# Band attention on one Trainium2 core: a fixed round order on three engines, the division a round later, low parts on GpSimd

## The chip, the cores and the metric

One core of one Trainium2 chip runs the whole program, launched once. The metric is device time in microseconds (us). The matrix engine is TensorE (PE; its weight loads are PEld), the others are VectorE (DVE), ScalarE (ACT) and GpSimd (POOL); SyncE (SP) issues the DMAs.

## The reference

One step of a hybrid encoder layer on 2048 prompt frames and 8 running streams of 16 frames. A combined projection feeds three mixers: band attention (8 heads of 64), a delta-rule mixer and a diagonal state-space mixer. Their outputs go through one output projection and a layer norm, then through a feed-forward block. The part at issue is the attention:

```python
def one_chunk(c):                      # prompt: 64 queries, their own chunk and the 8 chunks before
    s = jnp.einsum('bqhd,bkhd->bhqk', qc, kc) * scale + bias
    s = jnp.where(valid, s, NEG_INF)
    p = jax.nn.softmax(s, axis=-1)
    return jnp.einsum('bhqk,bkhd->bqhd', p, vc)

def band_attention_sample(q, k, v, k_cache, v_cache, table):   # 8 streams, 512 + 16 keys
    s = jnp.einsum('bqhd,bkhd->bhqk', q, kk) * d_h ** -0.5 + rel_bias(table, rel)
    return jnp.einsum('bhqk,bkhd->bqhd', jax.nn.softmax(s, axis=-1), vv)
```

## The kernel before

The program has stages: the combined projection; the mix stage, in which the state-space part (product `s5p`, L1020) ends; the attention; the output projection with its norm; the feed-forward block. The attention is the stretch from 913 to 1254 us of the trace.

A float32 product on PE is made from two parts of an operand: a high part, which is a cast to the type fp32r, and a low part, which is the operand minus its high part. So each 128-row block of queries and keys needs casts and subtractions before PE can take it.

`attention` (L1071) walks over 16 tiles of 128 queries, each with four pairs of heads: 64 rounds. A tile sees `nk` = min(i+1, 5) blocks of 128 keys. For a round:

- `a_scores` (L1160): for each of the two heads, and for each key segment (one segment up to tile 3, then mostly two, since keys lie in tiles of four blocks), PE multiplies high and low queries with the keys into a PSUM tile `aps` (L1184, L1185; four such tiles exist). DVE adds the bias `nb` and keeps a running extremum in `st` (`tensor_tensor_reduce`, below TTR, L1186; in the trace `CUSTOM_DVE_ANT_0` and a `DVE_READ_ACCUMULATOR2_ANT` behind it). ACT takes the exponential of a whole head and sums it (L1189, an `ACTIVATE` and its read of the accumulator). In the same function DVE inverts the two sums (L1191) and multiplies both heads (L1194, `TENSOR_SCALAR`, below TS).
- `a_values` (L1197): PE transposes the weights block by block (L1212) into `tps` tiles (three exist); the copies to `PT` go to ACT and DVE in turn (L1215, L1217); PE multiplies with the values (L1220) into the one PSUM tile `aob`; behind a tile's fourth pair ACT copies it out (L1223).

`a_values` is called `AHEAD` = 2 rounds behind `a_scores`. `a_tile` loads and splits the queries of a tile (casts on ACT L1155, L1156; low part `qlz` on DVE L1157). `a_kblock` does it for four key blocks at once (cast on ACT L1133, low part on DVE L1134). In tiles 1 to 8 `a_sample` does the attention of one running stream: scores (L1269), TTR (L1270), exponential (L1272), division (L1273, L1274), transposes (L1278), copy of `sPT` on ACT (L1279), then 20 short value products in a burst into the same `aob` tile (16 at L1289 and 4 at L1290), and two DVE copies into `sos` (L1293). In tiles 2 to 9 `w_part` splits an eighth of the output weights: two ACT casts (L61) and two DVE subtractions (L62).

The order on each engine is not the order of the text. A scheduler places instructions by priority and readiness: the order written is a preference, and an instruction that is ready later is passed by others. Each engine then runs its own list strictly in order.

Of the kernel before, what the change touches and what calls it, by code (L numbers as in the profile page):

```python
# [30 lines left out]
AHEAD = 2  # L31
# [11 lines left out]
class K:  # L43
# [1027 lines left out]
    def attention(self, es):  # L1071
# [17 lines left out]
        self.kst, self.vt = {}, {}  # L1089
# [6 lines left out]
        todo = []  # L1096
        for i in range(16):
            t = self.a_tile(i)
            for p in range(4):
                todo.append((t, p, self.a_scores(t, p)))  # L1100
                if len(todo) > AHEAD:
                    self.a_values(*todo.pop(0))
            if 2 <= i <= 9:
                self.w_part(i - 2)
            if 1 <= i <= 8:
                self.a_sample(i - 1)
                if i == 8:
                    nc.sync.dma_start(self.mixT[0:512, SEQ:NT].rearrange("(f p) t -> p f t", p=128), self.sos)

        w0 = c.tile([128, 5, 8, 128], F32, name="w0", tag="nb")  # L1110
        for x in todo:
            self.a_values(*x)
# [4 lines left out]

    def tsplit(self, parts, t):
        src, sl = self.at_a(parts, t)
        return src[:, sl].rearrange("(f p) t -> p f t", p=128)  # L1120

    def a_kblock(self, b):

        nc = self.nc
        ks = self.ak.tile([128, 8, 512], F32R, name="kst", tag="kst")
        for i in range(4):
            kr = self.ak.tile([128, 4, 128], F32, name="kr", tag="kr", bufs=2)
            nc.sync.dma_start(kr, self.tsplit(self.kT, b * 4 + i))
            ts = slice(i * 128, (i + 1) * 128)
            for q in range(2):  # L1130
                r, o = slice(q * 64, q * 64 + 64), slice(64 - q * 64, 128 - q * 64)
                hi = ks[r, q::2, ts]
                nc.scalar.copy(hi, kr[r])  # L1133
                nc.vector.tensor_tensor(ks[o, q::2, ts], kr[r], hi.bitcast(F32), OP.subtract)  # L1134
        self.kst[b] = ks

    def a_tile(self, i):

        nc = self.nc
        V = nc.vector  # L1140
        aw = self.aw
        b, r = divmod(i, 4)
        if r == 0:
            self.a_kblock(b)
        v = aw.tile([128, 512], F32, name="vt", tag="vt", bufs=6)
        vsrc, sl = self.at_a(self.vS, i)
        nc.sync.dma_start(v, vsrc[sl])
        self.vt[i] = v
        qr = aw.tile([128, 4, 128], F32, name="qr", tag="qr", bufs=2)
        nc.sync.dma_start(qr, self.tsplit(self.qT, i))  # L1150
        qd = aw.tile([128, 8, 128], F32R, name="qd", tag="qd")
        ql = self.qlz[i % 2]
        for q in range(2):
            rr, o = slice(q * 64, q * 64 + 64), slice(64 - q * 64, 128 - q * 64)
            nc.scalar.copy(qd[rr, q::2], qr[rr])  # L1155
            nc.scalar.copy(qd[o, q::2], qr[rr])  # L1156
            V.tensor_tensor(ql[rr, q::2], qr[rr], qd[rr, q::2].bitcast(F32), OP.subtract)  # L1157
        j0 = max(0, i - 4)
        return dict(i=i, qd=qd, ql=ql, vt=[self.vt[j] for j in range(j0, i + 1)], kst=dict(self.kst), ob=None)

    def a_scores(self, t, p):

        nc = self.nc
        V, mm = nc.vector, nc.tensor.matmul
        aw = self.aw
        i, qd, ql, kst = t["i"], t["qd"], t["ql"], t["kst"]
# [6 lines left out]
        for q in range(2):  # L1173
# [4 lines left out]
            if n1:  # L1178
                segs.append((kst[b - 1], min(512 - 128 * n1, 320), 512, 512 - 128 * n1, 0, 128 * n1))
            segs.append((kst[b], 0, max(128 * n2, 192), 0, 128 * n1, 128 * n2))  # L1180
            low = 3e38
            for ks, c0, c1, d0, x0, n in segs:
                ps = self.asp.tile([128, 512], F32, name="aps", tag="s")
                mm(ps[:, c0:c1], qd[:, h], ks[:, h, c0:c1], start=True, stop=False)  # L1184
                mm(ps[:, c0:c1], ql[:, h], ks[:, h, c0:c1], start=False, stop=True)  # L1185
                V.tensor_tensor_reduce(x[:, x0:x0 + n], ps[:, d0:d0 + n], nb[:, x0:x0 + n], 1.0, low,  # L1186
                                       OP.add, OP.min, st[:, q:q + 1])
                low = st[:, q:q + 1]
            nc.scalar.activation(x, x, AF.Exp, scale=-1.0, bias=st[:, q:q + 1], accum_out=st[:, 2 + q:3 + q])  # L1189
        rs = aw.tile([128, 2], F32, name="rs", tag="ars", bufs=4)  # L1190
        V.reciprocal(rs, st[:, 2:4])  # L1191
        for q in range(2):
            x = P[:, q, 0:128 * nk]
            V.tensor_scalar(x, x, rs[:, q:q + 1], None, OP.mult)  # L1194
        return P

    def a_values(self, t, p, P):  # L1197
        nc = self.nc
        V, mm = nc.vector, nc.tensor.matmul
        aw = self.aw  # L1200
        i, vt = t["i"], t["vt"]
        nk = len(vt)
        if t["ob"] is None:
            t["ob"] = self.aop.tile([128, 4, 128], F32, name="aob", tag="o")
        ob = t["ob"]
        PT = aw.tile([128, 10, 128], F32, name="PT", tag="PT")
        units = [(q, j) for j in range(nk) for q in range(2)]
# [627 lines left out]
```

## Time and profile before

| what | us |
|---|---|
| device time, median of three runs (lowest, highest) | 2910.81 (2909.86, 2921.8) |
| device time of the profiled execution | 2915.03 |
| its span, first to last instruction | 2913.2 |
| mean granted TensorE clock over the span | 0.986 of full speed |
| attention stage, 915.4 to 1254 | 338.6 |

The profile is one execution. A table of stretches gives an engine's busy time and the granted clock in each; a timeline gives an engine's instructions in order, and in brackets how long the engine stood idle before one and what released it; the waits sum such idle time by the line that ended it.

### The profile page before, as it was taken

Reading aid. Unit: us, or ns where it says so; the run is one execution under the profiler, and the core shown is the slowest. Engines: PE = TensorE matmul, PEld = TensorE weight load, DVE = VectorE, ACT = ScalarE, POOL = GpSimd, SP = SyncE. Lnnn points to the kernel's source line nnn. Section 1 sums busy time; section 2 is a strip of 40 time slices with the busy share of each in tenths; the row PEclk is TensorE's granted clock in tenths of the full one; section 3 lists DMA queues with packets and bytes.
Section 4 is the critical chain, followed back from the end, with each engine's and each line's share of the span. In section 5 each row is a group of like instructions: output and inputs, shape, how many; then the busy total and the mean of one; then the engine's idle time right before and its main releaser. Section 6 shows DMA issues by size and latency. Waiting matters only on the chain.

```text
span 2913.2 us, 46312 instructions
## 1 busy us (share of the span) xinstructions
PE 2795.9 (96%) x16677; PEld 2447.0 (84%) x16677; DVE 1963.9 (67%) x4972; ACT 1319.0 (45%) x2735; POOL 1001.0 (34%) x906
## 2 busy tenths in 40 slices
PE   8999999989999999999999999999999999999998
PEld 8988888867777777778889899888989988888887
DVE  7587887797764667968855555565555556566666
ACT  3554454343456556722244344354434435444443
POOL 0011111241100000002454444446554554776774
PEclk9999999999999889999999999999999999999999
DMA  5644444464557442144542122143222214322321
GB/s 183 202 107 121 111 129 121 134 171 133 165 182 220 142 138 61 50 159 159 179 157 76 58 71 75 58 165 141 100 73 78 97 66 156 145 98 94 113 83 58
DMA packets 292428, 351.88 MB, mean 121 GB/s; under 512 B 85586, under 2 KB 218534, under 8 KB 291878
## 3 DMA queue, kind: packets, MB, share of 16 engines
q1 hardware_dynamic: 292198, 348.92, 37.9%
q8 instruction: 131, 2.15, 0.3%
q14 instruction: 99, 0.81, 0.1%
HBM read 276.58 MB, written 74.89 MB: 121 GB/s over the span
## 4 chain that ended last, share of the span: by engine, by line
PE 47%; POOL 6%; DMA 3%; DVE 2%; ACT 2%; issue 1%; SPq 0%; DVEq 0%; ACTq 0%; POOLq 0%
PE fdp L67 7%; PE fdp L68 7%; PE fdp L66 7%; POOL wu L1482 2%; DMA wur<-in_w_upL 2%; PE wops L66 2%; PE wops L67 2%; PE wops L68 2%; PE fupz L68 2%; PE fupv L66 2%; PE fupv L68 2%; PE fupv L67 2%; PE fupz L66 2%; PE fupz L67 2%; PE fupx L66 2%; PE fupx L67 2%
## 5 line engine op out<-in xcount | busy, mean ns | idle before, releaser
L1482 POOL TENSOR_TENSOR wu<-wur,wu 128x512 fp32r<-128x512 f32 x315 | 420.3, 1338 | 556.7 <-ACT wu L1481 544.3
L1600 DVE TENSOR_TENSOR fy<-fy,fdp 128x512 f32<-128x512 f32 x500 | 342.2, 686 | 268.5 <-PE fdp L68 266.9
L66 PE MATMUL fdp<-wdh,hh 128*128 128x512 f32 x1020 | 397.7, 390 | 2.0 <-DVE fy L1600 1.9
L1481 ACT CAST wu<-wur 128x512 fp32r<-128x512 f32 x315 | 194.1, 617 | 448.7 <-DMA wur<-in_w_upL 202.8
L68 PE MATMUL fdp<-wdh,hl 128*128 128x512 f32 x1020 | 397.1, 389 | 0.0
L67 PE MATMUL fdp<-wdl,hh 128*128 128x512 f32 x1020 | 397.1, 389 | 0.0
L66 PE MATMUL pps<-xh,wh 128*128 128x384 f32 (+2 forms) x800 | 280.6, 352 | 10.0 <-ACT xh L61 8.7
L67 PE MATMUL pps<-xl,wh 128*128 128x384 f32 (+2 forms) x800 | 279.3, 349 | 2.1 <-DVE xl L62 2.0
L68 PE MATMUL pps<-xh,wl 128*128 128x384 f32 (+2 forms) x800 | 277.5, 348 | 0.4 <-DVE wl L62 0.3
L66 PEld LDWEIGHTS fdp<-wdh,hh 128*128 128x128 f32 x1020 | 191.4, 188 | 41.7 <-DVE fy L1600 3.7
L68 PEld LDWEIGHTS fdp<-wdh,hl 128*128 128x128 f32 x1020 | 191.5, 188 | 40.3 <-DVE hl L1547 0.2
L67 PEld LDWEIGHTS fdp<-wdl,hh 128*128 128x128 f32 x1020 | 191.5, 188 | 37.9 <-DVE wdl L62 0.2
L1547 DVE TENSOR_TENSOR hl<-fre,hh 128x384 fp32r<-128x384 f32 (+1 forms) x180 | 155.4, 864 | 89.8 <-ACT hh L1546 88.1
L61 ACT CAST wdh<-wdr 128x1024 fp32r<-128x1024 f32 x94 | 98.5, 1050 | 207.3 <-PE fdp L68 205.0
L66 PEld LDWEIGHTS pps<-xh,wh 128*128 128x128 f32 x800 | 152.1, 191 | 22.0 <-ACT xh L61 9.7
L67 PEld LDWEIGHTS pps<-xl,wh 128*128 128x128 f32 x800 | 152.0, 190 | 14.0 <-DVE xl L62 5.1
L68 PEld LDWEIGHTS pps<-xh,wl 128*128 128x128 f32 x800 | 151.8, 190 | 11.7 <-issue 1.8
L62 DVE TENSOR_TENSOR wl<-wr,wh 128x512 fp32r<-128x512 f32 (+1 forms) x152 | 104.7, 695 | 61.4 <-ACT wh L61 60.6
L62 DVE TENSOR_TENSOR wdl<-wdr,wdh 128x1024 fp32r<-128x1024 f32 x94 | 133.4, 1421 | 15.7 <-ACT wdh L61 15.7
L1447 POOL TENSOR_TENSOR fxc<-fxs 128x256 f32<-128x256 f32 x17 | 19.2, 1129 | 321.4 <-ACT fxs L1443 321.4
L61 ACT CAST wh<-wr 128x512 fp32r<-128x512 f32 (+1 forms) x152 | 92.5, 619 | 80.1 <-DMA wr<-in_w_inA 41.4
L1542 ACT ACTIVATE fre<-fre,ld_b_up 128x384 f32<-128x384 f32 (+1 forms) x144 | 85.9, 597 | 74.3 <-DVE fre L1551 48.4
(555 smaller groups left out, 7410.7 us busy)
## 6 DMA issues: line engine op xcount, KB each, us to landing
wdr<-in_w_dnL SPq DMA_DIRECT2D x96, 512.0 KB
wur<-in_w_upL SPq DMA_DIRECT2D x92, 512.0 KB
wr<-in_w_inA SPq DMA_DIRECT2D x70, 512.0 KB
TU<-tD SPq DMA_DIRECT2D x34, 256.0 KB
y<-in_x SPq DMA_DIRECT2D x17, 512.0 KB
x<-y SPq DMA_DIRECT2D x17, 512.0 KB
fxr<-x SPq DMA_DIRECT2D x17, 512.0 KB
fy<-x SPq DMA_DIRECT2D x17, 512.0 KB
```

The lines of the kernel that those rows point to most:

```text
L61: nc.scalar.copy(hi, src)
L62: nc.vector.tensor_tensor(lo, src, hi.bitcast(F32), OP.subtract)
L66: mm(out, lh, rh, start=first, stop=False, **kw)
L67: mm(out, lh, rl, start=False, stop=False, **kw)
L68: mm(out, ll, rh, start=False, stop=last, **kw)
L1447: P.tensor_tensor(b["T1"], b["B12"], b["B11"], OP.subtract)
L1481: self.nc.scalar.copy(hi, src)
L1482: P.tensor_tensor(lo, src, hi.bitcast(F32), OP.subtract)
L1542: nc.scalar.activation(r, src, AF.Relu, bias=self.bu[:, c * 2 + i:c * 2 + i + 1])
L1547: V.tensor_tensor(hl, r, hh.bitcast(F32), OP.subtract)
L1600: V.tensor_tensor(y, y, ps[x], OP.add)
```

## The change

What it does, in six parts:

1. The helpers `mm`, `turn`, `dve` and `act` put each attention instruction of PE, DVE and ACT behind the instruction that was written before it for the same engine (`behind`, with `issue_after`). So from the second round on these three engines run the order of the text. `w_part` and GpSimd's work are not pinned themselves.
2. A round k is written so: division of round k-1 (`a_norm`), scores of k, values of k-2 (`a_values`), transposes and copies of k-1 (`a_turn`).
3. The low parts of queries and keys go from DVE to GpSimd (`a_queries`, `a_keys`).
4. Key tiles are two fixed ones; a key block is loaded and split one block a tile, two tiles ahead, where four came at once. Queries come one tile ahead.
5. The sample's work is spread over its tile: scores at p = 0, division behind that round's scores, transposes at p = 1, the value burst at p = 2 before that round's scores. The caches of the next stream are loaded as soon as the last ones were read.
6. The copy of a tile's result, the casts and the exponentials keep their engines.

```diff
-                todo.append((t, p, self.a_scores(t, p)))
-                if len(todo) > AHEAD:
-                    self.a_values(*todo.pop(0))
-            if 2 <= i <= 9:
-                self.w_part(i - 2)
-            if 1 <= i <= 8:
-                self.a_sample(i - 1)
+                if p == 0:
+                    if i < 14:
+                        self.a_load_k(i + 2)
+                    if i < 15:
+                        self.a_load_q(i + 1)
+                elif p == 1 and i < 14:
+                    self.a_keys(i + 2)
+                elif p == 2 and i < 15:
+                    t1 = self.a_tile(i + 1)
+                    self.a_queries(t1, 0)
+                elif p == 3 and i < 15:
+                    self.a_queries(t1, 1)
+                if rounds:
+                    self.a_norm(rounds[-1])
+                if streams and p == 0:
+                    sample = self.s_scores(b)
+                    if b < 7:
+                        self.s_load_k(b + 1)
+                if streams and p == 2:
+                    self.s_values(b, sample)
+                    if b < 7:
+                        self.s_load_v(b + 1)
+                rounds.append(self.a_scores(t, p))
+                if streams and p == 0:
+                    self.s_norm(sample)
+                if len(rounds) > 2:
+                    self.a_values(rounds.pop(0))
+                if len(rounds) > 1:
+                    self.a_turn(rounds[0])
+                self.pinned = True
+                if streams and p == 1:
+                    self.s_turn(sample)
+                if p == 3 and 2 <= i <= 9:
+                    self.w_part(i - 2)
...
+    @contextmanager
+    def behind(self, engine):
+        last = next((i for i in reversed(self.nc.cur_bb.bb.instructions) if i.engine == engine), None)
+        if not self.pinned or last is None:
+            yield
+        else:
+            with self.tc.issue_after(last):
+                yield
+    def dve(self, f, *a, **kw):
+        with self.behind(mybir.EngineType.DVE):
+            getattr(self.nc.vector, f)(*a, **kw)
...
+    def a_keys(self, i):
+        kr, ks = self.ld_["k", i], self.kst[i // 4 % 2]
+        ts = slice(i % 4 * 128, i % 4 * 128 + 128)
+        for q in range(2):
+            r, o = slice(q * 64, q * 64 + 64), slice(64 - q * 64, 128 - q * 64)
+            hi = ks[r, q::2, ts]
+            self.act("copy", hi, kr[r])
+            self.nc.gpsimd.tensor_tensor(ks[o, q::2, ts], kr[r], hi.bitcast(F32), OP.subtract)
+    def a_queries(self, t, q):
+        qr, qd = self.ld_["q", t["i"]], t["qd"]
+        rr, o = slice(q * 64, q * 64 + 64), slice(64 - q * 64, 128 - q * 64)
+        self.act("copy", qd[rr, q::2], qr[rr])
+        self.nc.gpsimd.tensor_tensor(t["ql"][rr, q::2], qr[rr], qd[rr, q::2].bitcast(F32), OP.subtract)
+        self.act("copy", qd[o, q::2], qr[rr])
...
+    def a_norm(self, s):
+        P, st = s["P"], s["st"]
+        rs = self.aw.tile([128, 2], F32, name="rs", tag="ars", bufs=4)
+        self.dve("reciprocal", rs, st[:, 2:4])
+        for q in range(2):
+            x = P[:, q, 0:128 * s["nk"]]
+            self.dve("tensor_scalar", x, x, rs[:, q:q + 1], None, OP.mult)
```

The three places below are those on which the steps of the prediction rest. In the rows `ISA` is a TTR (with `aps` among its inputs) or its accumulator read. First DVE in one of the late tiles, before:

```order
L1191 RECIPROCAL rs<-st 128x2
L1186 ISA P,st<-aps,nb,st 128x384
L1186 ISA st 128x1
L1194 TENSOR_SCALAR P<-P,rs 128x640 x2
L1186 ISA P,st<-aps,nb,st 128x384
L1186 ISA st 128x1
L1217 COPY PT<-tps 128x512
L1157 TENSOR_TENSOR qlz_11564<-qr,qd 64x4x128
L1191 RECIPROCAL rs<-st 128x2
L1194 TENSOR_SCALAR P<-P,rs 128x640 x2
```

and now (the helper gives all of them one line, L1186):

```order
L1186 RECIPROCAL rs<-st 128x2
L1186 TENSOR_SCALAR P<-P,rs 128x640 x2
L1186 ISA P,st<-aps,nb 128x256
L1186 ISA st 128x1
L1186 ISA P,st<-aps,nb,st 128x384
L1186 ISA st 128x1
L1186 ISA P,st<-aps,nb 128x256
L1186 ISA st 128x1
L1186 ISA P,st<-aps,nb,st 128x384
L1186 ISA st 128x1
L1186 COPY PT<-tps 128x512
```

The low part has left the engine, and the division always stands ahead of all four TTRs of the next round, with the copy at the end. Second, PE around a sample's value burst in tiles 4 to 8, before:

```order
L1220 MATMUL aob<-PT,vt 64x128 x4
L1184 MATMUL aps<-kst,qd 128x512
L1220 MATMUL aob<-PT,vt 64x128 x2
L1185 MATMUL aps<-kst,qlz_11564 128x512
L1184 MATMUL aps<-kst,qd 128x192
L1185 MATMUL aps<-kst,qlz_11564 128x192
L1289 MATMUL aob<-sPT,sV 128x32 x4
L1290 MATMUL aob<-sPT,sVn 128x32
```

and now:

```order
L1178 MATMUL aob<-PT,vt 64x128 x10
L1182 MATMUL tps<-ld_c_ident,P 128x128 x10
L1182 MATMUL tps<-ld_c_ident,sP 128x128 x4
L1182 MATMUL tps<-ld_c_ident,sP 16x128
L1178 MATMUL aob<-sPT,sV 128x32 x4
L1178 MATMUL aob<-sPT,sVn 128x32
```

Scores stood directly ahead of the burst; now the round's transposes and the sample's own do, and the next scores come behind it. Third, ACT around the copy `sPT` that the burst needs, before:

```order
L1189 ACTIVATE P,st<-P,st 128x640 x2
L1272 ACTIVATE sP,sst<-sP,sst 128x528
L1189 ACTIVATE P,st<-P,st 128x640
L1279 COPY sPT<-tps 128x512
L1189 ACTIVATE P,st<-P,st 128x640
```

and now:

```order
L1190 CAST kst_11563<-kr 64x4x128 x2
L1190 ACTIVATE P,st<-P,st 128x640 x2
L1190 COPY aos<-aob 128x512
L1190 COPY PT<-tps 128x512
L1190 COPY PT<-tps 128x256
L1190 COPY sPT<-tps 128x512
L1190 CAST qd<-qr 64x4x128 x2
```

The copy now stands behind both exponentials of its round and three other copies.

## Rows read from the trace of the kernel before

**Rows 1.** The page's part 1: busy us (share of the span) xinstructions.

```profile
PE 2795.9 (96%) x16677; PEld 2447.0 (84%) x16677; DVE 1963.9 (67%) x4972; ACT 1319.0 (45%) x2735; POOL 1001.0 (34%) x906
```

**Rows 2.** Table of stretches (as its head): tile 0, tiles 1–3, 4–8, 9, 10–15.

```profile
core 0: us, PE busy (x) PEld busy (x) DVE busy (x) ACT busy (x) POOL busy (x), PEclk, DMA share, GB/s
915.40:923.30 7.90, 5.74 (x30) 4.24 (x30) 6.45 (x32) 5.42 (x22) 0.79 (x3) 0.67 0.72 239
923.30:979.90 56.60, 51.27 (x379) 39.21 (x378) 37.76 (x127) 37.02 (x91) 3.30 (x11) 0.87 0.51 164
979.90:1119.10 139.20, 132.34 (x1054) 105.60 (x1052) 99.41 (x312) 80.77 (x175) 3.73 (x13) 0.89 0.40 125
1119.10:1142.40 23.30, 23.22 (x219) 19.49 (x220) 17.93 (x58) 14.47 (x33) 0.00 (x0) 1.00 0.17 47
1142.40:1246.10 103.70, 96.38 (x857) 75.46 (x858) 92.67 (x290) 78.14 (x172) 0.00 (x0) 1.00 0.16 47
```

**Rows 3.** The waits in 913:1254: engine, line <- releaser: us, times, longest.

```profile
DVE sos L1293 <- PE aob L1290: 32.6, 8, 5.3
```

**Rows 4.** Timeline of DVE, tile 11: start us, us, op, [idle before <-releaser].

```profile
1163.76 0.17 DVE L1191 RECIPROCAL rs<-st 128x2 f32<-128x2 f32 x1 [0.56 <-ACT P L1189]
1163.96 1.02 DVE L1194 TENSOR_SCALAR P<-P,rs 128x640 f32<-128x640 f32 x2
1164.89 0.28 DVE L1186 CUSTOM_DVE_ANT_0 P<-aps,nb 128x128 f32<-128x128 f32 x1
...
1167.12 0.69 DVE L1217 COPY PT<-tps 128x512 f32<-128x512 f32 x1
1168.36 0.17 DVE L1191 RECIPROCAL rs<-st 128x2 f32<-128x2 f32 x1 [0.56 <-ACT P L1189]
```

**Rows 5.** The timeline of ACT beside it.

```profile
1166.12 0.83 ACT L1189 ACTIVATE P<-P,st 128x640 f32<-128x640 f32 x1 [1.01 <-DVE st L1186]
...
1166.95 0.56 ACT L1215 COPY PT<-tps 128x512 f32<-128x512 f32 x1
1167.41 0.83 ACT L1189 ACTIVATE P<-P,st 128x640 f32<-128x640 f32 x1
```

**Rows 6.** Groups by line and form in 913:1254: busy us, mean ns, idle before.

```profile
L1194 DVE TENSOR_SCALAR P<-P,rs 128x640 f32<-128x640 f32 x96 | 48.7, 548 | 0.5
...
L1157 DVE TENSOR_TENSOR qlz<-qr,qd 64x512 fp32r<-64x512 f32 x28 | 19.1, 682 | 0.7 <-ACT qd L1155 0.3
...
L1186 DVE CUSTOM_DVE_ANT_0 P<-aps,nb 128x384 f32<-128x384 f32 x32 | 17.4, 552 | 4.5 <-PE aps L1185 4.3
L1156 ACT CAST qd<-qr 64x512 fp32r<-64x512 f32 x28 | 17.3, 618 | 0.7
...
L1189 ACT ACTIVATE P<-P,st 128x384 f32<-128x384 f32 x8 | 4.9, 613 | 0.0
```

**Rows 7.** The timeline of PE in one sample's value matmuls.

```profile
1068.58 1.08 PE L1289 MATMUL aob<-sPT,sV 128*128 128x32 f32 x8
...
1069.71 1.06 PE L1289 MATMUL aob<-sPT,sV 128*128 128x32 f32 x8
...
1072.24 1.89 PE L1289 MATMUL aob<-sPT,sV 128*128 128x32 f32 x8
...
1074.37 0.77 PE L1184 MATMUL aps<-kst,qd 128*128 128x512 f32 x1
```

**Rows 8.** The timeline of DVE beside it.

```profile
1074.60 0.46 DVE L1293 COPY sos<-aob 64x64 f32<-64x64 f32 x2 [5.27 <-PE aob L1290]
1075.61 0.75 DVE L1186 CUSTOM_DVE_ANT_0 P<-aps,nb,st 128x512 f32<-128x512 f32 x1 [0.56 <-PE aps L1185]
```

**Rows 9.** Single lines of the last stage: duration ns min/median/max.

```profile
L1482 POOL TENSOR_TENSOR wu<-wur,wu x315: 1261/1294/2281, 1457.6 to 2862.3; 128x512 fp32r<-128x512 f32 x158
...
L1547 DVE TENSOR_TENSOR hl<-fre,hh x180: 477/780/1600, 1465.6 to 2863.7; 128x384 fp32r<-128x384 f32 x120, 128x320 fp32r<-128x320 f32 x60
```

**Rows 10.** The waits of PE in 770:913, the stage before.

```profile
PE s5p L1020 <- ACT kst L1133: 5.4, 2, 2.9
```

More of the change, by code (lines that the diff above doesn't have):

```diff
@@ L30 @@
 NDIAG = 4
-AHEAD = 2
 PACE1 = 2
@@ L1088, in attention @@
         nc.gpsimd.memset(nb[64:128, :, 0:64], 1e30)
-        self.kst, self.vt = {}, {}
+        self.vt, self.ld_ = {}, {}
+        self.kst = [c.tile([128, 8, 512], F32R, name=f"kst{i}") for i in range(2)]
+        for k in self.kst:
+            nc.gpsimd.memset(k[:, :, 128:192].bitcast(F32), 0.0)
         self.qlz = [c.tile([128, 8, 128], F32R, name=f"qlz{i}") for i in range(2)]
@@ L1095, in attention @@
         self.sample_setup(es)
-        todo = []
+        self.pinned = False
+        for k in range(2):
+            self.a_load_k(k)
+            self.a_keys(k)
+        self.a_load_q(0)
+        t = self.a_tile(0)
+        for q in range(2):
+            self.a_queries(t, q)
+        rounds = []
+        sample = None
+        self.s_load_k(0)
+        self.s_load_v(0)
         for i in range(16):
-            t = self.a_tile(i)
+            b = i - 1
+            streams = 0 <= b < 8
+            t1 = None
@@ L1110, in attention @@
         w0 = c.tile([128, 5, 8, 128], F32, name="w0", tag="nb")
-        for x in todo:
-            self.a_values(*x)
+        self.a_norm(rounds[-1])
+        self.a_values(rounds.pop(0))
+        self.a_turn(rounds[0])
+        self.a_values(rounds.pop(0))
         self.y0 = self.wp.tile([128, 8, 128], F32, name="y0", tag="wor")
@@ L1116, in attention, with mm, turn, act @@
         self.w_tile(0, self.y0, h, l, lambda: self.asp.tile([128, 512], F32, name="aps", tag="s"))
+    @contextmanager
[6 more added lines that the diff above has]
+                yield
+    def mm(self, *a, **kw):
+        with self.behind(mybir.EngineType.PE):
+            self.nc.tensor.matmul(*a, **kw)
+    def turn(self, out, src):
+        with self.behind(mybir.EngineType.PE):
+            self.nc.tensor.transpose(out, src, self.ident)
+    def dve(self, f, *a, **kw):
+        with self.behind(mybir.EngineType.DVE):
+            getattr(self.nc.vector, f)(*a, **kw)
+    def act(self, f, *a, **kw):
+        with self.behind(mybir.EngineType.Activation):
+            getattr(self.nc.scalar, f)(*a, **kw)
     def tsplit(self, parts, t):
@@ L1120, in tsplit @@
         return src[:, sl].rearrange("(f p) t -> p f t", p=128)
[L1122 to L1135, printed above, removed]
@@ new lines, in a_keys @@
+    def a_keys(self, i):
[6 more added lines that the diff above has]
+            self.nc.gpsimd.tensor_tensor(ks[o, q::2, ts], kr[r], hi.bitcast(F32), OP.subtract)
+    def a_tile(self, i):
+        v = self.vt[i] = self.aw.tile([128, 512], F32, name="vt", tag="vt", bufs=6)
+        vsrc, sl = self.at_a(self.vS, i)
+        self.nc.sync.dma_start(v, vsrc[sl])
+        qd = self.aw.tile([128, 8, 128], F32R, name="qd", tag="qd")
+        j0 = max(0, i - 4)
+        return dict(i=i, qd=qd, ql=self.qlz[i % 2], vt=[self.vt[j] for j in range(j0, i + 1)], ob=None)
@@ L1183, in a_scores, with a_turn @@
                 ps = self.asp.tile([128, 512], F32, name="aps", tag="s")
[L1184 to L1187, printed above, removed]
+                self.mm(ps[:, c0:c1], qd[:, h], ks[:, h, c0:c1], start=True, stop=False)
+                self.mm(ps[:, c0:c1], ql[:, h], ks[:, h, c0:c1], start=False, stop=True)
+                self.dve("tensor_tensor_reduce", x[:, x0:x0 + n], ps[:, d0:d0 + n], nb[:, x0:x0 + n], 1.0, low,
+                         OP.add, OP.min, st[:, q:q + 1])
                 low = st[:, q:q + 1]
-            nc.scalar.activation(x, x, AF.Exp, scale=-1.0, bias=st[:, q:q + 1], accum_out=st[:, 2 + q:3 + q])
-        rs = aw.tile([128, 2], F32, name="rs", tag="ars", bufs=4)
-        V.reciprocal(rs, st[:, 2:4])
-        for q in range(2):
[L1193 to L1207, printed above, removed]
+            self.act("activation", x, x, AF.Exp, scale=-1.0, bias=st[:, q:q + 1], accum_out=st[:, 2 + q:3 + q])
+        return dict(t=t, p=p, P=P, st=st, nk=nk)
+    def a_norm(self, s):
+        P, st = s["P"], s["st"]
+        rs = self.aw.tile([128, 2], F32, name="rs", tag="ars", bufs=4)
+        self.dve("reciprocal", rs, st[:, 2:4])
+        for q in range(2):
+            x = P[:, q, 0:128 * s["nk"]]
+            self.dve("tensor_scalar", x, x, rs[:, q:q + 1], None, OP.mult)
+    def a_turn(self, s):
+        P = s["P"]
+        PT = s["PT"] = self.aw.tile([128, 10, 128], F32, name="PT", tag="PT")
+        units = s["units"] = [(q, j) for j in range(s["nk"]) for q in range(2)]
         for u in range(0, len(units), 4):
@@ L1235, in sample_setup @@
         nc.gpsimd.tensor_scalar(nb, rv[:, ::-1], -1.0, None, OP.mult)
-        self.sQ = [c.tile([128, 4, 32], F32, name=f"sQ{i}") for i in range(1)]
-        for q in self.sQ:
-            nc.gpsimd.memset(q, 0.0)
+        self.sQ = c.tile([128, 4, 32], F32, name="sQ")
+        nc.gpsimd.memset(self.sQ, 0.0)
         self.sos = c.tile([128, 4, 128], F32, name="sos")
```

124 lines of the change are left out of this document (64 added, 60 removed).

## The prediction, made before the change was run

> **What bounds the kernel now.** I read the page's busy times first: PE is busy 96% of the span, so the kernel as a whole lives on PE [rows 1]. The change touches only the attention, and there the share is lower, so I then cut that stage by tiles [rows 2]. Read the columns us, PE busy and PEclk. Tiles 10 to 15, with five key blocks and no sample work, take 103.7 us for 23 rounds, 4.5 us a round, and PE is busy 96.4 of them at the full clock. Tiles 1 to 8 run at 0.87 and 0.89 of the clock: the clock has two levels, full and half, so 1 - 0.89 = 0.11 of the mean is 0.22 of the time at the low level. Over tiles 0 to 8 that is 5.2 + 14.7 + 30.6 = about 50 us at the low level, worth up to 25 us, since what PE computes there takes half as long at the high one. So in tiles 1 to 8 the stage is set partly by PE's clock, and in tiles 10 to 15 by something that nearly keeps up with PE.
>
> That something is seen in the timeline of DVE [rows 4]. The two RECIPROCALs are 4.60 us apart, and DVE waits 0.56 us for ACT's exponential before each. One turn of this loop is: invert, multiply two heads, four TTRs, then ACT's second exponential, then invert again. The order is exactly that which the change prescribes for all rounds, so the trace of before already holds a sample of the new round. Third view, the sample's work: in the waits DVE stands 32.6 us, eight times, for the value burst [rows 3], and the timelines of PE and DVE show one of them [rows 7, 8].
>
> **The sum, part by part,** against the profiled execution's 2915.03 us (the median of before is 0.15% below it; I scale at the end). A difference under about 0.5%, 14.6 us, can't be told from none by a measurement of this kernel.
>
> *Late tiles (10 to 15).* In the fixed order a round is a cycle from DVE to ACT and back: RECIPROCAL 0.20 and two TS 0.93 by their start times, TTRs from 1164.89 to 1167.12 = 2.23, together 3.36; then the second exponential and its accumulator read. In the sample that exponential starts 0.29 behind the last TTR (1167.41 against 1167.12), because a PT copy stands ahead of it [rows 5]; the new order puts the copies behind both exponentials. I take 0.12 in its place, and 0.95 from its start to the next RECIPROCAL (1168.36 - 1167.41). Sum 4.43 us. That is under today's 4.5 by only 0.08: 23 rounds give 101.9 for 103.7, **-1.8**. If the copy's 0.17 isn't won, 4.60 and +2.1; these are the bounds. The low parts that leave DVE (28 of queries at 0.68 us, 19 us of work [rows 6], and those of keys) bring next to nothing here, because the cycle in the sample holds none of them.
>
> *Tile 9* has today 23.3 us with output-weight work; four rounds of 4.43 and some 1.2 of that work left in the cycle give 19, **-4.3**.
>
> *Tiles 4 to 8.* Four rounds 17.7. The sample's scores and division add 1.3 on DVE at p = 0: two TTRs of 264 columns, some 0.4 each by the 552 ns of 384 [rows 6], and the division lies mostly inside the wait for the exponential. The two subtractions of the output weights are the size of a query's low part, 0.68 each, 1.4 to 1.5 for two. Then the burst. ACT's copy of sPT now stands behind both exponentials, the result copy and two PT copies. Counted from the RECIPROCAL of round p = 1, the exponentials end at 4.43, four copies take 1.8: 6.2, that is 1.8 into round p = 2. PE has by then been through scores, values and transposes, some 3.3 us of work, so it idles about 2.9 us ahead of the burst. The burst takes 4.5 us at the full clock, four quarters of 1.13 as the first, from 1068.58 to 1069.71, and 2.13 a quarter at the low one, as the last quarter did, from 1072.24 to 1074.37 [rows 7]. DVE is held behind it: the copies into sos come ahead of the round's TTRs. The first TTR comes at 1.8 + 4.5 + 0.65 = 6.95 where it would be at 1.13: **+5.8** a tile. (Before, a like wait cost 4.1 in the mean, 32.6 / 8, but scores already queued went on.) Without any effect on the clock a tile is 17.7 + 1.3 + 1.5 + 5.8 = 26.3, five are 131.6, against 139.2 today.
>
> *The clock.* What it does with the idle ahead of the burst no row of before shows. What shows is that a burst of short matmuls, with nothing idle ahead of it, loses the clock within it: its first quarter ran at 1.08 for eight matmuls, the last at 1.89 [rows 7]. Bounds: nothing changes (0), or the whole burst runs at half and the round behind it too, 4 + 3 = 7 us a sample. I take half of that, **3.6 a sample**, since idle time and a burst now follow each other where only the burst stood. Five tiles: 131.6 + 18 = 149.6, **+10.4** against 139.2.
>
> *Tiles 1 to 3.* The cycle with three blocks is 0.20 + 0.65 + 2 x 0.55 + 0.12 + 0.70 = 2.8 (TTR 552 ns, exponential 613 [rows 6]); with four, scaled by width, 3.3; with two, ACT is longer at 2.6. Four rounds each, with the same 7.1 (tile 1, no output weights) and 8.6: 17.5 + 19.7 + 21.8 = 59.0 plus three times 3.6 = 69.8 against 56.6, **+13.2**. *Tile 0*: ACT's casts of the next queries and keys (six at 0.62 [rows 6]) beside its exponentials give 2.4 a round, 9.6 against 7.9, **+1.7**.
>
> *The stage before.* Two blocks of four keys, 16 casts, are taken early on ACT, and PE waited twice for them, 5.4 us in all, 2.9 at the longest [rows 10]. Only two keys, 4 casts, are written that early now; I take one wait and its follow-up, **-4** (bounds 0 and -7).
>
> *At nothing*: the key and value fetches, which move on SP's queue ahead of their use by a tile or more, DMA engines being busy 0.16 to 0.51 of tiles 1 to 15 [rows 2]; GpSimd's low parts, 1.3 us each by its smallest comparable instruction [rows 9], some 5 us a tile on an engine that is busy at most 3.7 us in any of the stretches [rows 2]. What is queued behind them is the memset of sPT's tail, whose reader comes a round later. If that cover fails, rival 3. The drain behind tile 15 and the later stages hold the same instructions.
>
> Sum: -1.8 - 4.3 + 10.4 + 13.2 + 1.7 - 4 = **+15.2**, so 2930 for the profiled execution; by the ratio 2910.81 / 2915.03 a median of **2926 us**. Of the single terms, the burst's hold on DVE is the one that decides.
>
> **The rivals.**
>
> 1. *Faster: the clock keeps up.* The order that never lets short work pass long work could also leave PE's clock as it is or better. Then the 8 x 3.6 = 29 us vanish: 2926 - 29 = **2897**. For it: tiles 10 to 15, at 93% busy PE, hold the full clock throughout [rows 2], and the new rounds there are alike. Against it: PE's share falls in tiles 1 to 8 through the burst's wait. It decides if the granted clock of tiles 4 to 8 is at or above 0.89.
>
> 2. *The clock falls ahead of the burst and stays down*: the upper bound of that term, 8 x (7 - 3.6) = 27 more: **2953**. For it: already without the idle time the burst ends at half rate. The Trainium skill's page "TensorE: Matmul & The Clock Gate", section "Why this matters for your kernels", says the same as a rule: no idle gaps of PE between bursts of matmuls, or its throughput falls. By that rule alone this rival would be the forecast; the trace of before bears it out only for the burst's end. Against it: ACT may be earlier at the copy of sPT than I count, and the gap shorter.
>
> 3. *GpSimd's low parts hold up DVE.* DVE's subtractions in the last stage run at 477 ns at the least and up to 1600 where GpSimd subtracts too, and GpSimd's own run from 1261 to 2281 [rows 9], so the two do get in each other's way. Here a round's two TS (548 ns [rows 6]) stand in the cycle; if a low part of 1.3 us held them, each of some 60 would add between 0.3 and 1 us: +18 to +60, so **2945 to 2985**. Against it: the casts that release GpSimd stand behind the PT copies, 1 to 2 us into a round, when DVE is at its TTRs, which read a bias from SBUF and the rest from PSUM. The Trainium skill's page "SBUF — State Buffer", section "Who interferes with whom", has the rule that DVE's multiplication by a scalar and GpSimd can lock each other out for a whole instruction, and that an instruction with one SBUF input does not contend. By that the TTRs would be untouched and the sum stands; no run here shows it so far.
>
> 4. *The order isn't the bound anywhere*, all of it hides behind PE: the stage stays at 338 and only the stage before wins its 4: **2907**, no change.
>
> **How the numbers follow.** The forecast, 2926, has 0.4; rival 1 0.25; rival 2 0.16; rival 3 0.09; rival 4 0.1. The forecast's own range is 2913 to 2940, from the bounds of the late tiles (+3.9), the stage before (-3 to +4) and half the clock's term. It lies across the line at 2925.4, more of it above: 0.22 slower and 0.18 same. Rival 1 lies at the other line, 2896.3: 0.15 faster, 0.10 same. Rival 4 gives 0.07 same and 0.03 faster, should the late tiles gain more than counted. Slower: 0.22 + 0.16 + 0.09 = 0.47; same: 0.18 + 0.10 + 0.07 = 0.35; faster: 0.15 + 0.03 = 0.18. The range that leaves out 2 in 10 goes from 2890, a little under rival 1, to 2957, a little over rival 2.
>
> **What the new profile would show.** Right: RECIPROCALs 4.4 to 4.6 us apart in tiles 10 to 15, with DVE's wait for the exponential at about 0.4 us; in each of tiles 1 to 8 one wait of DVE of 5 us or more that ends with the burst, and PE idle some 3 us ahead of it with ACT's copy of sPT as its releaser; the granted clock of tiles 4 to 8 at 0.8 to 0.86; GpSimd's low parts near 1.3 us, TS still near 0.55. Wrong: bursts that follow closely on PE's transposes, a granted clock above 0.9 in tiles 1 to 8, or TS of 1 us and more.

## The result, and the profile after the change

The changed kernel takes 2951.2 us in the median (2945.1 to 2958.2, four runs) where the kernel before takes 2916.3 beside it: a ratio of 1.0123, with a 95% interval of 1.0102 to 1.0145. It is slower by 1.2%. The profiled execution took 2951.13 us with a span of 2949.3, against 2915.03 and 2913.2: 36.1 us more.

The page's part 1 of the changed kernel:

```profile
PE 2799.7 (95%) x16677; PEld 2466.6 (84%) x16677; DVE 1934.0 (66%) x4908; ACT 1319.3 (45%) x2735; POOL 1083.8 (37%) x972
```

PE does the same 16677 matmuls in about the same busy time; DVE has 64 instructions less and POOL 66 more. The time went into standing still and into the clock. The table of stretches, cut at the same RECIPROCALs as [rows 2] (tile 0; 1 to 3; 4 to 8; 9; 10 to 15; the columns are those of [rows 2]):

```profile
917.80:932.50 14.70, 8.03 (x49) 4.75 (x50) 9.11 (x36) 9.76 (x30) 8.24 (x11) 0.65 0.64 194
932.50:1005.60 73.10, 62.92 (x447) 51.41 (x446) 39.84 (x131) 42.41 (x100) 18.22 (x21) 0.81 0.53 167
1005.60:1159.20 153.60, 136.38 (x1045) 116.90 (x1045) 90.96 (x286) 81.15 (x174) 31.24 (x31) 0.81 0.32 98
1159.20:1176.90 17.70, 14.92 (x152) 13.20 (x152) 14.89 (x48) 14.29 (x33) 5.17 (x4) 1.00 0.21 62
1176.90:1279.20 102.30, 86.91 (x866) 74.46 (x866) 85.62 (x276) 78.74 (x173) 23.30 (x18) 1.00 0.15 45
```

Where no sample is worked on (last two rows) the change is a little faster, 120.0 for 127.0, at the full clock. Where samples are worked on, tiles 1 to 8 take 226.7 for 195.8, and the granted clock is 0.81 where it was 0.87 and 0.89. The waits of the changed kernel in 913 to 1296 us, beside [rows 3]:

```profile
ACT P L1190 <- DVE st L1186: 109.4, 94, 9.7
...
DVE sos L1186 <- PE aob L1178: 50.3, 8, 6.9
...
PE aps L1178 <- POOL sQ L1327: 4.0, 1, 4.0
```

ACT stands 109.4 us for DVE's TTRs (36.6 before), and DVE 50.3 us for the eight value bursts (32.6 before). One of them, in tile 4, on PE:

```profile
1010.90 1.01 PE L1182 MATMUL tps<-ld_c_ident,sP 128*128 128x128 f32 x4 [2.46 <-DVE PT L1186]
1012.21 0.38 PE L1182 MATMUL tps<-ld_c_ident,sP 128*16 128x128 f32 x1 [0.29 <-DMA kr<-kT]
1012.97 1.92 PE L1178 MATMUL aob<-sPT,sV 128*128 128x32 f32 x8 [0.38 <-ACT sPT L1190]
...
1019.39 1.89 PE L1178 MATMUL aob<-sPT,sV 128*128 128x32 f32 x8
...
1021.52 0.77 PE L1178 MATMUL aps<-kst,qd 128*128 128x512 f32 x1
```

and on DVE:

```profile
1012.70 0.28 DVE L1186 COPY sPT<-tps 16x128 f32<-16x128 f32 x1 [1.25 <-PE tps L1182]
1012.90 0.14 DVE L1186 RECIPROCAL rs<-st 128x2 f32<-128x2 f32 x1
1013.08 2.06 DVE L1186 TENSOR_SCALAR P<-P,rs 128x640 f32<-128x640 f32 x2
1021.75 0.46 DVE L1186 COPY sos<-aob 64x64 f32<-64x64 f32 x2 [6.61 <-PE aob L1178]
1022.76 0.69 DVE L1186 CUSTOM_DVE_ANT_0 P<-aps,nb 128x512 f32<-128x512 f32 x1 [0.56 <-PE aps L1178]
...
1027.46 0.16 DVE L1186 RECIPROCAL rs<-st 128x2 f32<-128x2 f32 x1
```

PE stands 2.46 us ahead of the sample's transposes, for a PSUM tile that DVE's copy frees. Then the burst runs from 1012.97 until the next scores start at 1021.52, 8.55 us, every quarter at 1.9 for eight matmul records (two for each product of the text): the low clock level from its start. DVE's first TTR comes at 1022.76, and from one RECIPROCAL to the next it is 14.56 us where a plain round takes 4.43.

### The profile page after: what moved, and what is told of

Its sections match the earlier page's. It is cut to its first block, busy times and chain, and to the rows that moved or that the text cites. A ratio compares the mean times of both kernels' runs of the same rounds, so it can differ in the third digit from the quotient of the medians.

```text
span 2949.3 us, 46393 instructions
## 1 busy us (share of the span) xinstructions
PE 2799.7 (95%) x16677; PEld 2466.6 (84%) x16677; DVE 1934.0 (66%) x4908; ACT 1319.3 (45%) x2735; POOL 1083.8 (37%) x972
## 4 chain that ended last, share of the span: by engine, by line
PE 63%; DVE 13%; POOL 8%; DMA 7%; issue 5%; ACT 4%; SPq 1%; DVEq 0%; ACTq 0%; POOLq 0%
PE fdp L66 6%; PE fdp L67 6%; PE fdp L65 6%; PE aob L1178 4%; PE pps L67 3%; PE pps L66 3%; PE pps L65 3%; DVE P L1186 3%; POOL wu L1572 2%; DMA wur<-in_w_upL 2%; PE wops L66 2%; PE wops L65 2%; PE wops L67 2%; PE bqs L649 2%; PE fupz L67 2%
## 5 line engine op out<-in xcount | busy, mean ns | idle before, releaser
L66 PEld LDWEIGHTS pps<-xl,wh 128*128 128x128 f32 x800 | 152.1, 190 | 14.7 <-DVE xl L61 5.9
L1190 ACT ACTIVATE P<-P,st 128x640 f32<-128x640 f32 (+4 forms) x128 | 97.4, 761 | 109.7 <-DVE st L1186 109.4
```

Source lines behind the costliest of these rows:

```text
L66: mm(out, lh, rl, start=False, stop=False, **kw)
L1190: getattr(self.nc.scalar, f)(*a, **kw)
```

## The experiments

Theory A: the fixed order makes the engines wait for each other around the sample's value burst, and the idle time on PE brings more of the low clock level. Rival B: the bursts lose the clock by themselves, wherever they stand. Rival C: GpSimd's low parts hold up DVE. Every kernel below is compared with the kernel before in the same job.

| kernel | median us | ratio to before (95%) |
|---|---|---|
| the change | 2951.2 | 1.0123 (1.0102 to 1.0145) |
| burst behind the scores | 2931.1 | 1.0061 (1.0040 to 1.0081) |
| transposes ahead of the scores | 2938.3 | 1.0086 (1.0057 to 1.0115) |
| both moves | 2923.1 | 1.0029 (1.0016 to 1.0042) |
| filled idle time | 2937.5 | 1.0087 (1.0056 to 1.0117) |
| output weights' split pinned | 2977.5 | 1.0221 (1.0198 to 1.0244) |
| low parts back on DVE | 3028.3 | 1.0395 (1.0373 to 1.0417) |
| pins on PE alone | 2930.4 | 1.0056 (1.0037 to 1.0075) |
| no pins | 2902.6 | 0.9963 (0.9949 to 0.9977) |
| no pins, both moves | 2899.9 | 0.9950 (0.9935 to 0.9965) |
| no pins, low parts on DVE | 2908.9 | 0.9979 (0.9965 to 0.9993) |
| kernel before, low parts on GpSimd | 2917.5 | 1.0011 (1.0001 to 1.0022) |
| no pins, both moves, samples a tile later | 2889.3 | 0.9918 (0.9902 to 0.9935) |

**The burst's place.** Two moves of the sample's work in the pinned text, apart and together. The transposes (`s_turn`) go ahead of the scores of round p = 1, the burst (`s_values`) behind those of p = 2:

```diff
                     self.a_norm(rounds[-1])
+                if streams and p == 1:
+                    self.s_turn(sample)
...
-                if streams and p == 2:
-                    self.s_values(b, sample)
...
                 rounds.append(self.a_scores(t, p))
                 if streams and p == 0:
                     self.s_norm(sample)
+                if streams and p == 2:
+                    self.s_values(b, sample)
...
-                if streams and p == 1:
-                    self.s_turn(sample)
```

> The changed kernel with one edit: in round p = 2 the sample's value burst stands behind that round's scores (and ahead of the tile's own values) instead of ahead of them, on PE; with it the two sos copies stand behind the four TTRs on DVE. Theory A (the round p = 2 of a sample's tile is long, 12.4 to 14.6 us for tiles 3 to 8 where a plain one is 4.43, because DVE can't start its TTRs before the burst is over): TTRs and exponentials now lie beside the burst, 3 to 5 us less per sample, 25 to 40 us in all: 2911 to 2926. Rival B (the low clock that the sparse stretch brings is the whole of it, wherever the burst stands): at most 10 us, 2940 or more, bursts still at 7 us. Rival C (GpSimd's low parts hold DVE's multiplications): no change, 2951.

> The changed kernel with one other edit: the sample's transposes and the copy of sPT stand ahead of the scores and exponentials of round p = 1 instead of at its end, so that the copy no longer waits behind exponentials and copies on ACT, nor the transposes for a tps tile that DVE frees late. The burst keeps its place. Theory A: PE's idle ahead of the burst goes; the burst starts right behind the transposes of round p = 1, and DVE's wait for it (50.3 us in all) shrinks by 2 to 3 us a sample; if the idle was also what kept the clock low, bursts come down from 7.4 us in the mean to under 6: together 20 to 40 us, 2911 to 2931. Rival B: bursts lose the clock by themselves and stay at about 7 us; then 10 to 15 us, 2936 to 2941. Rival C: no change.

> Both edits at once: the sample's transposes ahead of the scores of round p = 1, its value burst behind those of round p = 2. Theory A: the gains add in part, since each shortens the same wait: 35 to 60 us, 2891 to 2916, DVE's wait for the burst under 20 us in all. Rival B: about as the second edit alone. Rival C: no change.

They give back 20, 13 and 28 us of the change's 35. By the time alone the first lies between A and B, the second within B's range, and the third 7 us short of A's but well under the second, which B excludes. The traces decide more: DVE's wait for the burst went from 50.3 to 32.2, 40.9 and 25.8 us, and the eight bursts, from the first matmul's start to the last one's end in the timeline, from 59.0 us in all to 48.8, 50.2 and 44.5 (41.9 before the change). Each is one profiled execution, and the first one's, 2937.9 us, is among its slowest. So the same 20 products a sample lose less of the clock when they stand elsewhere, 6.1, 6.3 and 5.6 us a burst where B wanted about 7; but A's gains were counted too large: with the transposes moved it wanted bursts under 6, with both moves a wait under 20, and neither came. Single bursts run at 4.5 to 4.7, wholly at the high level, but no order here brings all eight there. Rival C, which wanted no change, is out.

**The idle time and the clock.** PE gets useless work, 16 transposes of the identity into a PSUM tile that nothing reads:

```diff
                 if streams and p == 1:
+                    ps = self.asp.tile([128, 512], F32, name="aps", tag="s")
+                    for z in range(16):
+                        self.turn(ps[:, z % 4 * 128:z % 4 * 128 + 128], self.ident)
                     self.s_turn(sample)
```

> The changed kernel with 16 transposes of the identity added on PE at the end of round p = 1, into a spare PSUM tile that nothing reads, ahead of the sample's transposes, where PE otherwise stands idle for up to 2.5 us. It does more work, 2.1 us a sample at the full clock. If it is the idle time ahead of the burst that lets the clock fall, the bursts come down from 7.4 us in the mean to 5 or 5.5, and the whole is 5 to 15 us faster than the changed kernel, 2936 to 2946, in spite of the added work. If the burst loses the clock by itself (rival B), bursts stay at 7 us and the whole is 0 to 15 us slower, 2951 to 2966.

2937.5, 13.7 less than the change, with more work: all four times lie below the change's four, though the intervals of the two ratios overlap by a little. The stretch of tiles 4 to 8 of this kernel:

```profile
999.70:1142.30 142.60, 133.99 (x1130) 116.52 (x1128) 87.86 (x284) 80.38 (x171) 31.53 (x31) 0.88 0.33 100
```

Clock 0.88 for 0.81, 142.6 us for 153.6. The bursts came to 48.9 us, 6.1 each, three of them at 4.65, wholly at the high level; not down to the 5 to 5.5 expected. So the idle time costs clock, and it is not all: the other five bursts, with no more than 1.2 us idle directly ahead of any, still took 6.2 to 7.8.

**Unpinned work between pinned work.**

```diff
-            self.split(self.woh[:, k, ns], self.wol[:, k, ns], wr[:, ns])
+            self.act("copy", self.woh[:, k, ns], wr[:, ns])
+            self.dve("tensor_tensor", self.wol[:, k, ns], wr[:, ns], self.woh[:, k, ns].bitcast(F32), OP.subtract)
```

> The changed kernel with the output weights' split pinned too: its two casts on ACT and two subtractions on DVE stand at the end of round p = 3 instead of where the scheduler puts them, between TTRs and exponentials. Theory A in a second form (part of the long rounds p = 0 to 2 of tiles 4 to 8, up to 14.6 us, is that unpinned work delays the copies that release the burst's PSUM and sPT): round p = 2 comes down to 12 to 12.5 us in all sample tiles and the whole to 2930 to 2940. If the place of that work doesn't matter, the same work in another place: 2948 to 2955.

A miss: 26 us slower than the change. In tiles 4 to 8 the round p = 2 stayed at 13.7 to 15.6 us, and round p = 3 went to 6.9. That round alone, 2.5 us over 4.43 in six of the eight tiles that do this work, makes up most of the 26: the work had lain largely beside waits where the scheduler put it, and pinned, it lengthens the cycle. That form of theory A falls.

**Low parts.** Back on DVE in the pinned order (`self.dve` for `self.nc.gpsimd` in `a_keys` and `a_queries`), and on GpSimd in the kernel before:

> The changed kernel with the low parts of queries and keys back on DVE, pinned into its order (two of keys at the head of round p = 1, one of queries at the heads of p = 2 and p = 3). Theory A (the fixed order and the burst's place cost the time): these 58 subtractions of 0.68 us now stand ahead of the division in a fixed order, 2.7 us a tile more in the cycle: 20 to 40 us slower than the changed kernel, 2971 to 2991. Rival C (GpSimd's low parts hold up DVE's multiplications, so that moving them cost more than it spared): at or below 2951.

> The kernel before with one part of the change alone: the low parts of queries and keys on GpSimd instead of DVE, nothing pinned. Theory A: DVE is freed of some 30 us that lie mostly beside other work: 0 to 12 us faster than before, 2901 to 2913, which would be most of what the unpinned version wins. Rival C: slower than before by 5 to 20 us, and multiplications of 0.65 us and more in the mean where they took 0.55.

The first is 77 us slower than the change, where 20 to 40 were expected. A row of DVE shows why, late in the stage, and the row of ACT that it waits for:

```profile
1230.82 0.68 DVE L1186 TENSOR_TENSOR qlz<-qr,qd 64x512 fp32r<-64x512 f32 x1 [2.12 <-ACT qd L1190]
```

```profile
1230.16 1.26 ACT L1190 CAST qd<-qr 64x512 fp32r<-64x512 f32 x2
```

A pinned low part costs not only its 0.68 us but also the 2.12 that DVE waits for a cast which stands behind ACT's copies. Over the stage that is 40 us of work and 51 us of such waits, and in tiles 10 to 12 a round with a low part takes 6.5 to 7.1 us, one without 4.43. In the kernel before, unpinned, the same part alone changes next to nothing (+0.1%), so theory A's 0 to 12 us weren't there either. Rival C is out in both, though in the second TS did rise to 600 ns in the mean, where it wanted 650 and more. What it was built on does happen: two TS took 2.06 us at 1013.08 above, where they take 1.02 elsewhere, with a low part of GpSimd starting at 1013.49. By the groups of the changed kernel:

```profile
L1186 DVE TENSOR_SCALAR P<-P,rs 128x640 f32<-128x640 f32 x96 | 51.9, 583 | 1.7
...
L1228 POOL TENSOR_TENSOR qlz<-qr,qd 64x512 fp32r<-64x512 f32 x30 | 41.9, 1398 | 155.0 <-ACT qd L1190 140.6 <-issue 14.2
```

583 ns for 548 [rows 6], 3.4 us over 96 of them, and 5.8 us over the TS of all widths (65.6 for 59.8). In the unpinned kernel below, which is faster than both, it is 606 ns.

**The pins.** All of them off (`behind` yields at once), those of DVE and ACT off, and the unpinned text with other edits:

> The changed kernel with the pins taken out: the text is in the same order, but the scheduler places PE's, DVE's and ACT's instructions freely, as in the kernel before; low parts stay on GpSimd, loads ahead, the division a round late. If the fixed order is what costs (theory A, its first step), the scheduler passes short work over the burst's wait and the time falls to 2905 to 2925. If low parts on GpSimd or the spread of the sample's work over the tile cost it, 2940 to 2955.

> The changed kernel with pins on PE alone; DVE and ACT are placed freely again. If it is PE's fixed order, the burst ahead of the scores, that costs: 2935 to 2951. If it is the strict order of DVE and ACT (a division that waits for an exponential while TTRs that are ready stand behind it, sPT's copy behind exponentials): 2903 to 2920, with late tiles under 17 us where the pinned ones take 17.7.

> The unpinned version with the low parts of queries and keys back on DVE. If the free order hides them as it did before, and the unpinned version's gain comes from the division a round later and from loads ahead: 2900 to 2908. If GpSimd's part is what wins: 2910 to 2925.

> The unpinned version with both edits in the text, the sample's transposes ahead of the scores of round p = 1 and its burst behind those of p = 2. With free placement the text only sets priorities, so I expect less than with pins: 0 to 10 us under the unpinned version's 2902.6, that is 2893 to 2903, and a version that beats both kernels. If the place in the text doesn't matter without pins: 2900 to 2906.

Without pins the same text takes 2902.6, 48.6 less than the change, better than its range and less than before: the fixed order is what costs, and the rest of the change is a gain. With low parts on DVE it is 2908.9, just between its two ranges: GpSimd's part of that gain may be 6 us, but the two intervals overlap. Pins on PE alone leave 2930.4, between its two ranges: releasing DVE and ACT is worth 21 us, releasing PE after that another 28. PE's part shows at the burst ahead of the scores: with PE alone pinned DVE still stands 47.7 us for the bursts, unpinned 30.2. DVE's and ACT's part is seen in round p = 1, which falls from 6.0 to 7.2 us to 4.1 to 4.9 in tiles 4 to 8. Pins on DVE or on ACT alone were not run. Tiles 1 to 3, 4 to 8 and 10 to 15 of the unpinned kernel:

```profile
932.00:990.30 58.30, 56.72 (x433) 45.52 (x433) 36.21 (x126) 36.96 (x89) 10.85 (x16) 0.85 0.60 187
990.30:1118.10 127.80, 123.38 (x1063) 105.01 (x1063) 89.28 (x293) 81.31 (x177) 29.57 (x31) 0.89 0.40 122
...
1133.30:1227.70 94.40, 87.44 (x866) 74.47 (x866) 82.53 (x274) 73.42 (x166) 19.13 (x14) 1.00 0.15 46
```

The sample tiles come back to 0.85 and 0.89 of the clock and PE is busy 97% there. The late tiles lie 8 us under the pinned ones. Both moves in the unpinned text give 2899.9, within the range and not to be told from the version without them.

**The first sample.** In the changed kernel PE waits once for a sample's queries, between tile 0 and tile 1, then SP's queue and GpSimd beside it:

```profile
928.10 1.99 PE L1178 MATMUL aps<-sK,sQ 128*32 128x264 f32 x16 [3.97 <-POOL sQ L1327]
```

```profile
921.04 0.37 SPq L1198 DMA_DIRECT2D kr<-kT  x1
...
922.83 0.50 SPq L1324 DMA_DIRECT2D sqr<-qT  x1
```

```profile
918.41 2.60 POOL L1212 TENSOR_TENSOR kst<-kr,kst 64x512 fp32r<-64x512 f32 x2 [8.72 <-ACT kst L1190]
```

The load of the queries, `sqr`, stands on SP's queue behind a key load that goes out at 921.04, just when GpSimd's low part of earlier keys ends (918.41 + 2.60); the waits of SP's queue put 3.7 us of waiting for that low part ahead of it. The run with low parts on DVE bears this out: there the key load goes out at 917.33, 3.7 us earlier, and PE waits 0.29 us for the first queries instead of 3.97. The last run puts the samples one tile later, without pins and with both moves:

```diff
-            b = i - 1
+            b = i - 2
...
-            if i == 8:
+            if i == 9:
```

> The unpinned version with both edits, and the samples' work in tiles 2 to 9 instead of 1 to 8. In the changed kernel the step from tile 0 to tile 1 takes 7.7 us where 2.4 was counted, because PE waits 4 us for the first stream's queries (a DMA that stands on SP's queue behind a key load, which waits for GpSimd). If that wait is what makes it long: the step comes down to 2 to 3 us and the whole to 2893 to 2898. If the sample's work only moves its cost to another tile: 2898 to 2903.

2889.3 us, better than its range, and a ratio of 0.9918: it beats both kernels. Its tiles 0 and 9:

```profile
922.00:929.60 7.60, 5.89 (x42) 4.45 (x43) 6.82 (x33) 6.73 (x25) 1.97 (x4) 1.00 0.73 216
...
1107.80:1130.20 22.40, 22.40 (x211) 20.43 (x211) 16.74 (x57) 14.60 (x32) 5.50 (x4) 0.92 0.20 60
```

Tile 0 takes 7.6 us for the change's 14.7, and for 14.0 in the run that it is to be compared with, the unpinned one with both moves. Tile 9, with a sample now, takes 22.4 for 15.8 there, tiles 1 to 3 take 53.5 for 59.2, and the attention from its first RECIPROCAL to its last 301.6 for 311.5. So the place of the samples is worth some 10 us. That it is the wait for the queries isn't shown by this run: in the run beside it PE waited only 0.5 us for them, and its step from tile 0 to tile 1 still took 8.2 us.

## Why the prediction was right, and where its steps failed

The sign and the range held, and the two things named as deciding, DVE held behind the burst and the clock, are what the runs showed. The size was too small: 15 us forecast, 36 in the profiles. The time lies above the forecast's own range of 2913 to 2940, next to rival 2's 2953, and it got there by another way than rival 2's. Of the 21 us that were missed, 5 lie in tile 0, 6 in the stage before and 3 behind the attention, in terms that have nothing to do with the burst; that the sum still fell within 2890 to 2957 is in part the luck of a wide range. Step by step, from the stretches above against [rows 2]:

| step | forecast | measured |
|---|---|---|
| late tiles | -1.8 | -1.4 |
| tile 9 | -4.3 | -5.6 |
| tiles 4 to 8 | +10.4 | +14.4 |
| tiles 1 to 3 | +13.2 | +16.5 |
| tile 0 | +1.7 | +6.8 |
| the stage before (start of tile 0) | -4 | +2.4 |
| behind tile 15 | 0 | +3.0 |

*Late tiles.* The cycle was right to the digit: it is 4.43 us, as worked out from the sample in the trace of before; two RECIPROCALs in tile 12 of the changed kernel, with DVE's wait of 0.39 us:

```profile
1208.40 0.17 DVE L1186 RECIPROCAL rs<-st 128x2 f32<-128x2 f32 x1 [0.39 <-ACT P L1190]
...
1209.53 0.68 DVE L1186 CUSTOM_DVE_ANT_0 P<-aps,nb 128x512 f32<-128x512 f32 x1
...
1210.37 0.35 DVE L1186 CUSTOM_DVE_ANT_0 P<-aps,nb,st 128x128 f32<-128x128 f32 x1
...
1211.76 0.69 DVE L1186 COPY PT<-tps 128x512 f32<-128x512 f32 x1
1212.83 0.17 DVE L1186 RECIPROCAL rs<-st 128x2 f32<-128x2 f32 x1 [0.39 <-ACT P L1190]
```

*Tiles 4 to 8.* The price of round p = 2 came out as counted, 5.8 + 3.6 = 9.4: from RECIPROCAL to RECIPROCAL the five take 69.3 us, 13.9 each, 9.4 over 4.43. But that is luck, for the parts were others. The burst doesn't start 1.8 us into the round: in tile 4 it starts 0.07 behind the RECIPROCAL (1012.97 against 1012.90), for round p = 1 had grown in its place. And it takes 7.7 us in the mean of these five, not 4.5. The step that failed is round p = 1, put at a plain 4.43: it takes 6.0 to 7.2, since DVE's small copy of sPT's tail stands ahead of the next RECIPROCAL and waits 1.25 us for PE (up to 1.85 in tile 5), which waits 2.46 for a PSUM tile. I had weighed ACT's queue there and not the ring of three `tps` tiles. With the transposes moved ahead of the scores that copy waits for nothing, and p = 1 takes 5.1 to 5.7. The five rounds p = 1 came to 32.2 us where 22.2 were counted; the tiles are only 4 us over because the 7.5 counted for the output weights' subtractions lie inside these rounds and not on top of them.

So a sign that the prediction gave for being wrong came true: in tiles 4 to 8 the burst follows closely on PE's transposes, 0.4 to 0.5 us, and the idle time lies ahead of the sample's transposes, 0.7 to 2.5 us, with DVE's copy to `PT` as its releaser. Only in tiles 1 to 3 does PE wait for ACT's copy of sPT as foretold, 2.1, 1.7 and 1.3 us.

*Tiles 1 to 3.* The same small copy of DVE waits here too, but for GpSimd, three times. Its row among the waits in 913 to 1296 us, under those of the two waits of PE just named:

```profile
PE aob L1178 <- ACT sPT L1190: 7.3, 8, 2.1
PE tps L1182 <- DVE PT L1186: 7.1, 6, 2.5
...
DVE sPT L1186 <- POOL sPT L1368: 4.4, 3, 2.3
```

The memset of sPT's tail stands behind the keys' low parts on GpSimd. The prediction had it at nothing, with a reader "a round later"; its reader, the small copy, comes in the same round. Round p = 1 takes 4.0, 4.0 and 4.5 us there where 2.6, 2.8 and 3.3 were counted.

*The clock* was taken at 3.6 us a sample between 0 and 7, and the fill run shows that PE's idle time has a share in it. Rival 2 was not the case as written, since only two of the eight bursts run at the low level from start to end. The rule of the Trainium skill's page "TensorE: Matmul & The Clock Gate", section "Why this matters for your kernels", against idle gaps between bursts points the right way: filling the gap raised the granted clock of tiles 4 to 8 from 0.81 to 0.88. It isn't the whole, for five bursts without such a gap fell to the low level all the same.

*Tile 0* failed on a term put at nothing: "the key and value fetches, which move on SP's queue ahead of their use". The first sample's queries are no fetch ahead, and GpSimd's low parts stand in front of them by way of the key load. The step to tile 1 takes 7.65 us where 2.4 was counted, 5 of the 6.8 us: PE's wait is 3.97 of it, and the rest is about what the sample's own scores take, which the forecast counts in tile 1. The last run wins some 10 us by placing the samples later, but by which wait stays open.

*The stage before* was forecast at -4 and measured at +2.4, but one execution can't decide it: in the six kernels with the same text up to there (all pins, low parts on GpSimd) the first RECIPROCAL stands anywhere from 909.4 to 918.0 us. PE's waits in 770 to 916 us, beside [rows 10]:

```profile
PE s5p L1057 <- DVE yq L1052: 6.3, 4, 2.5
PE s5p L1019 <- ACT kst L1190: 2.7, 1, 2.7
```

and a row of the kernel before:

```profile
PE s5p L1058 <- DVE yq L1053: 2.2, 5, 0.7
```

In this execution the wait for key casts is half as long, 2.7 for 5.4, as counted, but PE waits 6.3 us for DVE there where it waited 2.2. Why DVE is later wasn't tried; the other five kernels show 3.8 to 6.0. *Behind tile 15* the same instructions run; 3 us lies within the 13 us by which four runs of this kernel differ.

*Rival 3* stays out: the lock is seen, but on few of the TS, and it is worth 3 to 6 us of DVE's time and not 18 to 60. One such pair (2.04 us) stands in round p = 1 of tile 5, which takes 7.1 us where tiles 6 to 8 take 6.0. What GpSimd's low parts cost more is the queue behind them: the memset and, in tile 0, the key load. By the rule of the Trainium skill's page "SBUF — State Buffer", section "Who interferes with whom", the doubled TS pair at 1013.08 is what a lock between the two engines looks like; the trace agrees, with 2.06 us for 1.02.

## What to carry to other kernels

Price a fixed order not only by its cycle but at each place where a short instruction (here a copy of 0.28 us) stands ahead of the cycle's next step and waits for another engine: the cycle in the late tiles was exact, and what was missed in tiles 1 to 8 began at such a place. Ask also what stands behind moved work in its new engine's queue: here a memset of 0.2 us and a load. Before pinning, run the same text without pins; here the restructured text was a gain of 0.4% and the pins a loss of 1.6%. Work moved to an idle engine is worth what its place in the order makes of it: putting the same low parts on GpSimd saved 77 us in the pinned order, perhaps 6 without pins, and nothing in the kernel before.

## What the runs showed that was not expected

The unpinned late tiles run at 4.11 us a round, under the 4.43 that I had taken for the bound. One round of DVE there:

```profile
1153.99 0.17 DVE L1186 RECIPROCAL rs<-st 128x2 f32<-128x2 f32 x1 [0.57 <-ACT P L1190]
...
1155.12 0.28 DVE L1186 CUSTOM_DVE_ANT_0 P<-aps,nb 128x128 f32<-128x128 f32 x1
...
1155.33 0.29 DVE L1186 CUSTOM_DVE_ANT_0 P<-aps,nb 128x128 f32<-128x128 f32 x1
...
1155.54 0.75 DVE L1186 CUSTOM_DVE_ANT_0 P<-aps,nb,st 128x512 f32<-128x512 f32 x1
...
1156.21 0.75 DVE L1186 CUSTOM_DVE_ANT_0 P<-aps,nb,st 128x512 f32<-128x512 f32 x1
...
1156.88 0.69 DVE L1186 COPY PT<-tps 128x512 f32<-128x512 f32 x1
1158.10 0.17 DVE L1186 RECIPROCAL rs<-st 128x2 f32<-128x2 f32 x1 [0.53 <-ACT P L1190]
```

The scheduler takes both heads' first segments and then both second ones. A second TTR needs the extremum `st` of the first, and right behind it, as pinned, it starts 0.84 us after one of 0.68 (1209.53 to 1210.37). With the other head's TTR between, nothing is lost: four TTRs take 1.76 us (1155.12 to 1156.88) instead of 2.23 (1209.53 to 1211.76). That interleaving is the likely cause of the 4.11; it was read from the timelines and not tried by itself. The second surprise is how far the clock multiplies a wait: with low parts pinned on DVE all eight bursts ran at 8.73 or 8.74 us, the low level from start to end, and the granted clock was 0.70 in tiles 1 to 3 and 0.74 in tiles 4 to 8.
